# Memory attention of a sample group: split fp32r keys and values against unsplit fp32 in four column groups

## The chip, the core and the metric

The kernel runs on one core of one Trainium2 chip. The metric is device time in microseconds (us), the median of the runs of a kernel. A core has five engines that run side by side and meet at semaphores: TensorE (PE; its weight loads are shown as PEld), VectorE (DVE), ScalarE (ACT), GpSimd (POOL) and SyncE (SP), which here only starts transfers. Matmul results go to PSUM, of which eight banks of 128 x 512 fp32 exist in this program (the pool psp). All DMA queues share the core's 16 DMA engines.

## The reference, cut to what matters

One layer of a decoder is computed for a prompt of 256 tokens (TP) and a sample group of 8 sequences of 8 tokens (TS = 64 rows, NB = 8, LS = 8), with the same weights. The stage that changes is the cross-attention to 256 memory tokens per sequence, 4 heads of 512:

```python
def mem_attend(xn, k, v, wq, wo):
    q = (xn @ wq).reshape(b, L, MEM_HEADS, MEM_HEAD_DIM)
    s = jnp.einsum('blhd,bmhd->bhlm', q, k.astype(q.dtype)).astype(jnp.float32) * (1.0 / math.sqrt(MEM_HEAD_DIM))
    p = jax.nn.softmax(s, axis=-1)
    o = jnp.einsum('bhlm,bmhd->blhd', p.astype(v.dtype), v).reshape(b, L, D_MODEL)
    return (o @ wo).astype(xn.dtype)
```

For the prompt, k and v were computed earlier in the kernel and stand in DRAM (one sequence). For the sample they are inputs, cache_mem_k and cache_mem_v, eight sequences of 256 x 2048 fp32 each: a head of one sequence is 256 x 512, 512 KB.

## The kernel before, in words

**Precision.** TensorE takes fp32 operands in a slow form and fp32r operands (fewer mantissa bits) in a fast one. The kernel keeps fp32 accuracy by splitting a tile x into H = x as fp32r (an ACT copy) and L = x - H (a DVE subtraction), and by issuing three fp32r matmuls H*H, H*L, L*H for a product of two split operands. `split` (L246 to L249) does it; `high()` and `low()` give the buffers (seven each, HLB).

**The stream.** Work is fed to `Stream` (L58) as units of four parts: load (starts the weight DMA), first, second (preparations on DVE, ACT, POOL) and comp (matmuls). `add` runs a unit's load at once; the unit is prepared when more than `ahead` units stand behind it (WA = 3); its matmuls are issued when more than `room` prepared units of its kind wait (g for gemm units, a for attention units). Side generators (softmax, results) advance by one step with each unit whose matmuls are issued; `wait(n)` in them is n such steps. PE, ACT and DVE execute in exactly this program order.

**Units of the attention stage.** Four query panels qs (`panel`, L1095): 16 units of 128 rows of w_mem_q, each 12 matmuls of 320 columns (tile pg). The first panel runs alone; panels 1 to 3 stand between the keys of heads 0 to 2 (`between`). The first output panel o0, from w_mem_o, is handled in the same way around the keys of head 3 and the values after it. When a panel ends, `evac_q` (L1189) copies the queries out: the prompt's into qh and ql, the sample's, split, into qm, a zeroed matrix in which each sample's 8 query rows stand at their own columns, H beside L.

`kv_units` (L1275) makes two units of a 256 x 512 tile of keys or values. `kv_load` queues its load into one of four kv buffers (KVT): keys with four DMAs from SP, values with one from POOL; three are started ahead, then one with each tile used. For keys, DVE transposes 128 x 512 (tile tt, L1288). Then ACT makes KH (L1297) and DVE, or in 20 to 30% of the cases POOL (POOL_KV), makes KL (L1298). Prompt and sample go the same way.

`sample_scores` (L1321, tile pss): per sample and head, for each of four 128-wide pieces of the head, one matmul with KH and one with KL, 64 stationary columns from qm, 256 moving columns. `sample_softmax` adds the two halves with an fp32 matmul (psm), takes the softmax, transposes it and writes it, split, into pm (`split_diagonal`, L1178). `sample_values` (L1347, tile pso): two pieces of 128 tokens with VH and VL, 128 stationary columns of pm, 512 moving columns; `sample_result` adds up with another fp32 matmul (L1238). psp and po are the prompt's scores and values (three matmuls each). The values of a head run one head and LAG = 4 steps behind its keys; a step is one tile of keys and one of values.

After the stage, `residual_in` opens the next buffers and the rest of the output projection follows as ordinary gemm units (L367 to L369).

Of the kernel before, what the change touches and what calls it, by code (L numbers as in the profile page):

```python
# [57 lines left out]
class Stream:  # L58
# [105 lines left out]
def step(ctx, tc, ins, outs, dbg=None, stop=None):  # L164
# [79 lines left out]
    strm = Stream(WA, g=GD, a=KVB - 1)  # L244
# [15 lines left out]
    def rstd_of(pool, sq, n, count):  # L260
# [6 lines left out]
        t = pool.tile([P, n], F32, tag="rt", bufs=1, name="rt")  # L267
# [827 lines left out]
    def panel(w2d, c, ah, al, evac, wide=False):  # L1095
# [4 lines left out]
        def unit(k):  # L1100
# [20 lines left out]
            def comp():  # L1121
                if k == 0:
                    pts.extend(ps(f"pg{m}") for m in range(4))
# [15 lines left out]
    def open_tiles():  # L1139
# [3 lines left out]
        iv = ident.rearrange("p (b i q) -> p b i q", i=2, q=LS)  # L1143
        V.tensor_tensor(PQ["sel"].rearrange("p (b q) -> p b q", q=LS), iv[:, :, 0], iv[:, :, 1], ALU.add)
        PQ["half"] = pq.tile([TS, 2, TS], F32, name="half")
        zero = ident[0:TS, 0:TS].unsqueeze(1).broadcast_to([TS, 2, TS])
        S.activation(PQ["half"], zero, AF.Copy, scale=0.0)
        for g in range(2):
            V.tensor_copy(PQ["half"][:, g, 32 * g:32 * g + 32], PQ["sel"][0:TS, 0:32])
        for name, n, c in (("qm", 4, TS), ("pm", 2, P)):  # L1150
            t = pq.tile([P, n * NB, c], F32R, name=name)
            S.activation(t, ident[:, 0:c].unsqueeze(1).broadcast_to([P, n * NB, c]), AF.Copy, scale=0.0)
            PQ[name] = t
# [24 lines left out]
    def split_diagonal(t, src, n):  # L1178

        c = t.shape[2]  # L1180
        nb = c // 16
        for b0 in range(0, NB, nb):
            x = src[:, :, LS * b0:LS * (b0 + nb)].rearrange("p n (b q) -> p n b q", q=LS)
            hi, lo = (bass.AP(t.tensor, t.offset + c * b0 + LS * i, [list(t.ap[0]), [NB * c, n], [c + 16, nb], [1, LS]])
                      for i in range(2))
            S.activation(hi, x, AF.Copy)
            V.tensor_tensor(lo, x, hi.bitcast(F32), ALU.subtract)

    def evac_q(m, pt):  # L1189
        PQ.setdefault("parts", []).append(pt)  # L1190
        if m == 3:
            parts = PQ.pop("parts")
            qs = PQ["pool"].tile([P, 512], F32, tag="tt", bufs=TTB, name="qs")[:, 0:4 * TS].rearrange("p (j t) -> p j t", t=TS)
# [6 lines left out]
    def softmax(out, src, r):  # L1200
# [5 lines left out]
        V.scalar_tensor_tensor(m, m, -1.0, r, ALU.mult, ALU.mult)  # L1206
        for b in range(nb):
            S.activation(out[:, b], src[:, b], AF.Exp, bias=m[:, b:b + 1], scale=r[:, b:b + 1], accum_out=z[:, b:b + 1])
        V.reciprocal(z, z)
# [3 lines left out]
    def sample_softmax(sc, h):  # L1213
        pq = PQ["pool"]
        SC = pq.tile([P, 512], F32, tag="tt", bufs=TTB, name="SC")[0:TS]
        S.activation(SC, sc[0:TS], AF.Copy)
        yield from wait(3)
# [11 lines left out]
        split_diagonal(PQ["pm"], pt[:, 0:2 * TS].rearrange("p (m q) -> p m q", q=TS), 2)  # L1229
        yield 1  # L1230

    def sample_result(po, h):
        O = PQ["pool"].tile([P, 512], F32, tag="tt", bufs=TTB, name="O")
# [5 lines left out]
        split(AH[:, 4 * h:4 * h + 4, TP:T], AL[:, 4 * h:4 * h + 4, TP:T], pt[:, 0:4 * TS].rearrange("p (j t) -> p j t", t=TS))  # L1239
        yield 1  # L1240

    def prompt_softmax(sc, h):
        SP = PQ["pool"].tile([P, 2, TP], F32, tag="SP", bufs=1, name="SP")
        softmax(SP, sc.rearrange("p (b m) -> p b m", m=TP), PQ["r"][:, 0:2])
        yield from wait(6)
# [6 lines left out]
        split(PQ["ph"], PQ["pl"], pt.rearrange("p (m q) -> p m q", q=TP))  # L1252
        yield 1

    att_n = count(), count()
# [19 lines left out]
    def kv_units(src, keys, comp):  # L1275
# [4 lines left out]
        def unit(u):  # L1280
            def first():
                if u == 0:
                    next_load()
                    box["t"] = ready.popleft()
                t = box["t"]
                if keys:
                    tt = PQ["pool"].tile([P, 512], F32, tag="tt", bufs=TTB, name="tt")
                    V.transpose(tt.rearrange("p (k a i) -> p k a i", k=2, i=32),  # L1288
                                t.rearrange("p (a k j) -> p k a j", a=8, k=4)[:, 2 * u:2 * u + 2])
                    box[u] = tt  # L1290
                else:
                    box[u] = t[:, 512 * u:512 * u + 512]
# [128 lines left out]
    for _ in range(3):  # L1421
        strm.then(next_load)
# [700 lines left out]
```

## Time and profile before

| | us |
|---|---|
| median of 3 runs | 3209.01 (3207.13 to 3214.09) |
| profiled execution | 3211.91 |
| its span, first to last instruction | 3210.1 |
| busy: PE / DVE / ACT / POOL | 3138.9 / 2336.8 / 1631.5 / 1343.9 |
| mean granted TensorE clock | 0.989 |

Busy times are unions of what an engine executes. A matmul's busy time includes the way through the array and so overlaps with that of the next one; the pace of matmuls is read from start to start. An engine's idle time is put down to what ended it ("<-ACT KH L1297" is: until ACT had made KH). The granted clock falls for a while when TensorE has paused.

### The profile page before, as it was taken

The numbers are of one execution on the slowest core, as the hardware profiler recorded it, in microseconds if no ns is written. First come the engines' busy times: TensorE is split into PE (matmuls) and PEld (weight loads), VectorE is DVE, ScalarE is ACT, GpSimd is POOL, SyncE is SP. The second block draws the span as 40 slices with busy tenths as digits, with TensorE's granted clock in tenths as the row PEclk, the third lists the DMA queues.
The fourth block names the chain that finished last, engine by engine and source line by source line (L and its number), as shares of the span: only waits on it lengthen the run. The fifth ranks groups of instructions, "written<-read, shape, count | busy, mean of one in ns | idle before, by whom it ended". The sixth has DMA issues, their size and how long they took to land.

```text
span 3210.1 us, 57528 instructions
## 1 busy us (share of the span) xinstructions
PE 3138.9 (98%) x20589; PEld 2930.0 (91%) x20589; DVE 2336.8 (73%) x4551; ACT 1631.5 (51%) x3219; POOL 1343.9 (42%) x1438
## 2 busy tenths in 40 slices
PE   8999999999999999889999999999999999999997
PEld 7889999999999998779999999999999888888886
DVE  5556866666565557786688899987875888888885
ACT  6545543334454445555444444666664555555554
POOL 0002211111100001330138899988888555556552
PEclk9999999999999999989999999999999999999998
DMA  8668899899999988875676688878998989999995
GB/s 264 206 209 301 283 313 317 300 314 294 320 318 315 310 271 190 223 207 196 187 218 215 236 308 323 317 275 299 332 322 284 333 322 367 328 335 337 336 316 187
DMA packets 475372, 909.29 MB, mean 283 GB/s; under 512 B 40608, under 2 KB 286536, under 8 KB 449573
## 3 DMA queue, kind: packets, MB, share of 16 engines
q1 hardware_dynamic: 352972, 562.95, 52.7%
q0 software_dynamic: 54528, 208.44, 18.9%
q10 hardware_dynamic: 67584, 134.23, 12.3%
q8 instruction: 161, 2.64, 0.3%
q14 instruction: 127, 1.03, 0.1%
HBM read 849.41 MB, written 190.05 MB: 324 GB/s over the span
## 4 chain that ended last, share of the span: by engine, by line
PE 43%; DVE 2%; POOL 2%; issue 1%; DMA 1%; ACT 1%; DVEq 0%; POOLq 0%; SPq 0%; ACTq 0%
PE acc L2025 7%; PE acc L2026 7%; PE acc L2024 7%; PE pu L1871 6%; PE pu L1869 6%; PE pu L1870 6%; PE pgate L1775 2%; POOL L L1853 1%; DVE tt L1841 0%; PE pg L367 0%; PE pg L369 0%; PE pg L368 0%; DMA act_d<-at 0%; DVE gu L1733 0%; DVE L L249 0%
## 5 line engine op out<-in xcount | busy, mean ns | idle before, releaser
L249 DVE TENSOR_TENSOR L<-W,H 128x512 fp32r<-128x512 f32 x1320 | 912.0, 718 | 356.6 <-ACT H L248 350.7
L248 ACT ACTIVATE H<-W 128x512 fp32r<-128x512 f32 x1320 | 797.7, 625 | 673.9 <-PE acc L2026 237.3
L1853 POOL TENSOR_TENSOR L<-tt,H 128x512 fp32r<-128x512 f32 x509 | 645.1, 1297 | 76.6 <-ACT H L1850 67.8
L367 PE MATMUL pg<-AH,H 128*128 128x320 f32 (+1 forms) x1872 | 588.5, 314 | 1.7 <-ACT H L248 1.7
L1869 PE MATMUL pu<-XP,H 128*128 128x256 f32 x2048 | 585.6, 286 | 0.0
L1871 PE MATMUL pu<-XP,L 128*128 128x256 f32 x2048 | 580.4, 283 | 3.7 <-POOL L L1853 3.6
L369 PE MATMUL pg<-AH,L 128*128 128x320 f32 (+1 forms) x1872 | 579.7, 310 | 0.3 <-DVE L L249 0.3
L1870 PE MATMUL pu<-XP,H 128*128 128x256 f32 x2048 | 579.3, 283 | 0.0
L368 PE MATMUL pg<-AL,H 128*128 128x320 f32 (+1 forms) x1872 | 579.2, 309 | 0.0
L1841 DVE STREAM_TRANSPOSE tt<-W 128x512 f32<-128x512 f32 x512 | 338.1, 692 | 115.9 <-POOL L L1853 108.5
L2025 PE MATMUL acc<-L,wt 128*128 128x512 f32 x1024 | 399.0, 390 | 0.7 <-DVE L L249 0.6
L2024 PE MATMUL acc<-H,wt 128*128 128x512 f32 x1024 | 398.4, 389 | 0.0
L2026 PE MATMUL acc<-H,wt 128*128 128x512 f32 x1024 | 398.4, 389 | 0.0
L1871 PEld LDWEIGHTS pu<-XP,L 128*128 128x128 f32 x2048 | 392.7, 192 | 5.3 <-POOL L L1853 5.3
L1869 PEld LDWEIGHTS pu<-XP,H 128*128 128x128 f32 x2048 | 393.0, 192 | 0.2 <-issue 0.2
L1870 PEld LDWEIGHTS pu<-XP,H 128*128 128x128 f32 x2048 | 393.0, 192 | 0.0
L1850 ACT ACTIVATE H<-tt 128x512 fp32r<-128x512 f32 x512 | 307.0, 626 | 135.0 <-DVE tt L1841 105.1
L367 PEld LDWEIGHTS pg<-AH,H 128*128 128x128 f32 (+1 forms) x1872 | 351.2, 188 | 5.0 <-ACT H L248 2.2
L368 PEld LDWEIGHTS pg<-AL,H 128*128 128x128 f32 (+1 forms) x1872 | 351.4, 188 | 2.3
L369 PEld LDWEIGHTS pg<-AH,L 128*128 128x128 f32 (+1 forms) x1872 | 351.0, 187 | 1.5 <-DVE L L249 0.9
L1973 POOL TENSOR_TENSOR at<-at,G 128x108 f32<-128x108 f32 x192 | 165.3, 874 | 256.9 <-DMA at<-act_d 214.6
L2025 PEld LDWEIGHTS acc<-L,wt 128*128 128x128 f32 x1024 | 192.2, 188 | 42.7 <-DVE L L249 3.0
(485 smaller groups left out, 5291.7 us busy)
## 6 DMA issues: line engine op xcount, KB each, us to landing
u_d<-in_peer_u_dram ACTq DMA_DIRECT2D x128, 1024.0 KB
W<-u_d SPq DMA_DIRECT2D x128, 1024.0 KB
W<-in_peer_v_dram SPq DMA_DIRECT2D x256, 512.0 KB
W<-in_w_in_dram SPq DMA_DIRECT2D x176, 512.0 KB
W<-in_w_out_dram SPq DMA_DIRECT2D x64, 512.0 KB
W<-in_w_mem_k_dram SPq DMA_DIRECT2D x32, 512.0 KB
W<-in_w_mem_v_dram SPq DMA_DIRECT2D x32, 512.0 KB
W<-in_w_mem_q_dram SPq DMA_DIRECT2D x32, 512.0 KB
```

Of the source, the lines that this page charges most:

```text
L248: S.activation(h, src, AF.Copy)
L249: V.tensor_tensor(l, src, h.bitcast(F32), ALU.subtract)
L367: PE.matmul(out, hv[:, j, c0:c1], ah[:, k, 0:n], start=st, stop=False)
L368: PE.matmul(out, hv[:, j, c0:c1], al[:, k, 0:n], start=False, stop=False)
L369: PE.matmul(out, lv[:, j, c0:c1], ah[:, k, 0:n], start=False, stop=sp)
L1853: G.tensor_tensor(l, src, h.bitcast(F32), ALU.subtract)
L1869: PE.matmul(pu[:, 0:TP], hv[:, j], PP["xp"][:, 0, k], start=k == 0, stop=False)
L1870: PE.matmul(pu[:, 0:TP], hv[:, j], PP["xp"][:, 1, k], start=False, stop=False)
L1871: PE.matmul(pu[:, 0:TP], lv[:, j], PP["xp"][:, 0, k], start=False, stop=k == KC - 1)
L2024: PE.matmul(out, th, h, start=i == 0, stop=False)
L2025: PE.matmul(out, th, l, start=False, stop=False)
L2026: PE.matmul(out, tl, h, start=False, stop=i == P - 1)
```

## The change

The sample's keys and values are no longer split. Keys are transposed as a whole tile (128 x 1024, `turned`) and values are used as they were loaded; both go to TensorE as fp32, against fp32 queries (qm) and probabilities (pm) of 32 columns. The four 128-wide pieces of a head's keys are multiplied into four groups of 32 PSUM partitions (32j to 32j + 32), and so are the two token halves of two samples' values. A sample pair's values are issued when the second tile is there. The matrix half, now 128 rows, and sel add the groups up. The prompt's tiles are still split, into the common H and L buffers and without POOL. qm exists twice, for even and odd heads; SC and O share a buffer of their own. The softmax generators pause between their steps. Nine kv buffers take the place of four, four loads are started ahead in place of three; LAG is 3; within the stage five units stand ahead and room g is 4; room a is 2, later 3. Four units of o0 move ahead into the keys of head 3. A small buffer of `rstd_of` (rt) shares that of sq.

```diff
-HLB, KVB, GD, WA, WB = 7, 5, 6, 3, 4
-TU, AB, TTB, KVT, OB = 5, 3, 3, 4, 3
+HLB, GD, WA, WB = 7, 6, 3, 4
+TU, AB, TTB, KVT, OB = 5, 3, 3, 9, 3
-DW, XW, LAG = 8, 5, 4
+DW, XW, LAG = 8, 5, 3
-POOL_KV = 0.2, 0.3
+Q_AHEAD, Q_ROOM, KV_AHEAD = 5, 4, 4
...
-        if len(self.loading) > self.ahead:
+        while len(self.loading) > self.ahead:
...
-    strm = Stream(WA, g=GD, a=KVB - 1)
+    strm = Stream(WA, g=GD, a=2)
...
-        t = pool.tile([P, n], F32, tag="rt", bufs=1, name="rt")
+        t = pool.tile([P, n], F32, tag="sq", bufs=1, name="rt")
...
-        for name, n, c in (("qm", 4, TS), ("pm", 2, P)):
-            t = pq.tile([P, n * NB, c], F32R, name=name)
...
+        PQ["half"] = clear("half", [P, 2, TS])
+        V.tensor_reduce(PQ["half"][:, 0, 0:32], ident.rearrange("p (g r) -> p r g", r=32), AX.X, ALU.add)
+        V.tensor_copy(PQ["half"][:, 1, 32:64], PQ["half"][:, 0, 0:32])
+        PQ["qm"] = [clear(f"qm{i}", [P, 4 * NB, 32]) for i in range(2)]
+        PQ["pm"] = clear("pm", [P, 2 * NB, 32])
...
-                S.activation(qs[:, j], part[:, TP:T], AF.Copy)
-            split_diagonal(PQ["qm"], qs, 4)
+                S.activation(diagonal(PQ["qm"][h % 2], j, [[128, 2], [40, 4]]),
+                             part[:, TP:T].rearrange("p (a b q) -> p a b q", a=2, q=LS), AF.Copy)
...
         V.scalar_tensor_tensor(m, m, -1.0, r, ALU.mult, ALU.mult)
+        yield from wait(2)
         for b in range(nb):
             S.activation(out[:, b], src[:, b], AF.Exp, bias=m[:, b:b + 1], scale=r[:, b:b + 1], accum_out=z[:, b:b + 1])
+        yield from wait(2)
         V.reciprocal(z, z)
...
-        SC = pq.tile([P, 512], F32, tag="tt", bufs=TTB, name="SC")[0:TS]
-        S.activation(SC, sc[0:TS], AF.Copy)
-        yield from wait(3)
+        SC = pq.tile([P, 512], F32, tag="SO", bufs=1, name="SC")
+        S.activation(SC, sc, AF.Copy)
+        yield from wait(2)
...
-        SN = pq.tile([TS, 1, TP], F32, tag="SN", bufs=1, name="SN")
-        softmax(SN, pt[0:TS, 0:TP].unsqueeze(1), PQ["r"][0:TS, 2:3])
-        yield from wait(6)
+        yield 1
+        SN = nrm.tile([P, TP], F32, tag="ms", bufs=1, name="SN")[0:TS].unsqueeze(1)
+        yield from softmax(SN, pt[0:TS, 0:TP].unsqueeze(1), PQ["r"][0:TS, 2:3])
+        yield from wait(2)
...
-        split_diagonal(PQ["pm"], pt[:, 0:2 * TS].rearrange("p (m q) -> p m q", q=TS), 2)
+        for u in range(2):
+            S.activation(diagonal(PQ["pm"], u, [[72, 4], [32, 2]]),
+                         pt[:, u * TS:(u + 1) * TS].rearrange("p (x y q) -> p x y q", y=2, q=LS), AF.Copy)
...
-        O = PQ["pool"].tile([P, 512], F32, tag="tt", bufs=TTB, name="O")
+        O = PQ["pool"].tile([P, 512], F32, tag="SO", bufs=1, name="O")
...
-        softmax(SP, sc.rearrange("p (b m) -> p b m", m=TP), PQ["r"][:, 0:2])
-        yield from wait(6)
+        yield from softmax(SP, sc.rearrange("p (b m) -> p b m", m=TP), PQ["r"][:, 0:2])
+        yield from wait(3)
...
+    def next_tile():
+        next_load()
+        return ready.popleft()
+
+    def turned(t):
+        tt = PQ["pool"].tile([P, 1024], F32, tag="tt", bufs=TTB, name="tt")
+        V.transpose(tt.rearrange("p (k a i) -> p k a i", k=4, i=32), t.rearrange("p (a k j) -> p k a j", a=8, k=4))
+        return tt
...
             def second():
-                h, l = (PQ["pool"].tile([P, 512], F32R, tag=x, bufs=KVB, name=x) for x in ("KH", "KL"))
-                src = box.pop(u)
-                S.activation(h, src, AF.Copy)
-                (G if spread(next(att_n[keys]), POOL_KV[keys]) else V).tensor_tensor(l, src, h.bitcast(F32), ALU.subtract)
-                box["hl", u] = h, l
+                h, l = high(), low()
+                split(h, l, box["t"][:, 512 * u:512 * u + 512])
+                box[u] = h, l
...
         def sample_scores(b):
-                for j in range(2):
-                    q = PQ["qm"][:, (2 * u + j) * NB + b]
-                    for i, kk in enumerate((kh, kl)):
-                        PE.matmul(out, q, kk[:, TP * j:TP * j + TP], start=b % 4 == 0 and u == j == i == 0,
-                                  stop=b % 4 == 3 and u == j == i == 1)
+            kv_load(cache_k[0, b, :, h], True)
+            def first():
+                st["k", b] = turned(next_tile())
+            def comp():
+                tt = st.pop(("k", b))
+                for j in range(4):
+                    PE.matmul(st["ss"][32 * j:32 * j + 32, TP * (b // 4):TP * (b // 4) + TP], PQ["qm"][h % 2][:, j * NB + b],
+                              tt[:, TP * j:TP * j + TP], start=b % 4 == 0, stop=b % 4 == 3)
...
         def sample_values(b):
-                for i, vv in enumerate((vh, vl)):
-                    PE.matmul(st["so"], PQ["pm"][:, u * NB + b], vv, start=b == u == i == 0, stop=b == NB - 1 and u == i == 1)
+            def unit(i):
+                kv_load(cache_v[0, i, :, h], False)
+                def first():
+                    st["v", i] = next_tile()
+                def comp():
+                    if i == b:
+                        return
+                    vs = [st.pop(("v", n)) for n in (b, i)]
+                    for y, v in enumerate(vs):
+                        for u in range(2):
+                            g = 2 * y + u
+                            PE.matmul(st["so"][32 * g:32 * g + 32], PQ["pm"][:, u * NB + b + y], v[:, 512 * u:512 * u + 512],
+                                      start=b == 0, stop=b == NB - 2)
+                return None, first, None, comp, "a"
+            return [unit(b), unit(b + 1)]
...
-        between[3 * nk + LAG + 1 + i] = o0[2 * i:2 * i + 2]
-        between[4 * nk + LAG + 1 + 2 * i] = o0[8 + i:9 + i]
+        between[3 * nk + i] = o0[i:i + 1]
+        between[3 * nk + LAG + 1 + i] = o0[4 + i:5 + i]
+        between[4 * nk + LAG + 2 + 2 * i] = o0[8 + i:9 + i]
...
-                for u in range(2):
-                    steps += ks[u:u + 1] + bs[u:u + 1] + vs[u:u + 1]
-    for _ in range(3):
+            steps += ks + bs[:1] + vs + bs[1:]
+        if n == nk + LAG + 3:
+            steps.append(lambda: strm.room.update(a=3))
+    strm.then(lambda: strm.room.update(g=Q_ROOM))
+    strm.ahead = Q_AHEAD
+    for _ in range(KV_AHEAD):
         strm.then(next_load)
...
+    strm.ahead = WA
+    strm.then(lambda: strm.room.update(g=GD))
```

More of the change, by code (lines that the diff above doesn't have):

```diff
@@ L1093, in step, with panel @@
     strm.then(open_q)
-    def panel(w2d, c, ah, al, evac, wide=False):
+    def panel(w2d, c, ah, al, evac, wide=False, need=()):
         pts, box, units = [], {}, []
@@ L1121, in comp @@
             def comp():
+                assert all((n, k // 4) in done for n in need)
                 if k == 0:
@@ L1142, in open_tiles, with clear @@
         PQ["sel"] = pq.tile([P, TS], F32, name="sel")
[L1143 to L1149, printed above, removed]
-        for name, n, c in (("qm", 4, TS), ("pm", 2, P)):
-            t = pq.tile([P, n * NB, c], F32R, name=name)
-            S.activation(t, ident[:, 0:c].unsqueeze(1).broadcast_to([P, n * NB, c]), AF.Copy, scale=0.0)
-            PQ[name] = t
+        iv = ident.rearrange("p (y u x q) -> p y u x q", y=2, u=2, q=LS)
+        V.tensor_tensor(PQ["sel"].rearrange("p (x y q) -> p y x q", y=2, q=LS), iv[:, :, 0], iv[:, :, 1], ALU.add)
+        def clear(name, shape):
+            t = pq.tile(shape, F32, name=name)
+            S.activation(t, ident[:, 0:shape[2]].unsqueeze(1).broadcast_to(shape), AF.Copy, scale=0.0)
+            return t
+        PQ["half"] = clear("half", [P, 2, TS])
[3 more added lines that the diff above has]
+        PQ["pm"] = clear("pm", [P, 2 * NB, 32])
         PQ["qh"] = pq.tile([P, 4, TP], F32R, name="qh")
@@ L1176, in step, with diagonal, evac_q @@
     strm.then(open_tiles)
[L1178 to L1189, printed above, removed]
+    def diagonal(t, n, steps):
+        return bass.AP(t.tensor, t.offset + 32 * NB * n, [list(t.ap[0]), *steps, [1, LS]])
+    def evac_q(m, pt, h):
         PQ.setdefault("parts", []).append(pt)
@@ L1239, in sample_result @@
         split(AH[:, 4 * h:4 * h + 4, TP:T], AL[:, 4 * h:4 * h + 4, TP:T], pt[:, 0:4 * TS].rearrange("p (j t) -> p j t", t=TS))
+        done.add(("res", h))
         yield 1
@@ L1252, in prompt_softmax @@
         split(PQ["ph"], PQ["pl"], pt.rearrange("p (m q) -> p m q", q=TP))
+        done.add(("ph", h))
         yield 1
-    att_n = count(), count()
     loads = deque()
@@ L1273, in next_load, with prompt_units @@
             loads.popleft()()
-    def kv_units(src, keys, comp):
+    def next_tile():
[5 more added lines that the diff above has]
+        return tt
+    def prompt_units(src, keys, comp):
         kv_load(src, keys)
@@ L1381, in evac_o @@
         evac_next(XN["x"], k, pt, norm_sum(2), 4, BH, BL)
-    qs = [panel(w_mem_q[0], c, BH, BL, evac_q, wide=True) for c in range(4)]
-    o0 = panel(w_mem_o[0], 0, AH, AL, lambda m, pt: evac_o(m, pt))
+    qs = [panel(w_mem_q[0], c, BH, BL, lambda m, pt, c=c: evac_q(m, pt, c), wide=True) for c in range(4)]
+    o0 = panel(w_mem_o[0], 0, AH, AL, lambda m, pt: evac_o(m, pt), need=("res", "pv"))
     def residual_in():
@@ L1407, in step @@
             vs = tile_units(1, n - nk - LAG)
-            ks = tile_units(0, n)
-            if vs or n == 0:
-                steps += vs + ks[:1] + bs[:1] + ks[1:] + bs[1:]
-            else:
-                steps += bs + ks
+            steps += vs + bs + tile_units(0, n)
         else:
@@ L1415, in step @@
             vs = tile_units(1, n - nk - LAG)
-            if n < 4 * nk and n % nk == NB:
-                steps += ks + bs + vs
-            else:
-                for u in range(2):
-                    steps += ks[u:u + 1] + bs[u:u + 1] + vs[u:u + 1]
-    for _ in range(3):
+            steps += ks + bs[:1] + vs + bs[1:]
[4 more added lines that the diff above has]
+    for _ in range(KV_AHEAD):
         strm.then(next_load)
     for u in qs[0] + steps + o0[12:14]:
-        strm.add(*u)
+        if callable(u):
+            u()
+        else:
+            strm.add(*u)
+    strm.ahead = WA
+    strm.then(lambda: strm.room.update(g=GD))
     strm.then(residual_in)
```

45 lines of the change are left out of this document (18 added, 27 removed).

## The prediction

> **What bounds the kernel now.** I read the page first. TensorE is busy nearly throughout and the chain that ended last is mostly TensorE, so time is gained only where TensorE waits or where it is given less to stream. The clock line dips once, near the middle.
>
> ```profile
> span 3210.1 us, 57528 instructions
> PE 3138.9 (98%) x20589; PEld 2930.0 (91%) x20589; DVE 2336.8 (73%) x4551; ACT 1631.5 (51%) x3219; POOL 1343.9 (42%) x1438
> PEclk9999999999999999989999999999999999999998
> PE 43%; DVE 2%; POOL 2%; issue 1%; DMA 1%; ACT 1%; DVEq 0%; POOLq 0%; SPq 0%; ACTq 0%
> ```
>
> Next the timeline gave the borders of the attention stage (first matmul of the query panel, L1128; first matmul of the gemm behind the panels, L367), and the table by stretches its inside (columns after the span: busy time of PE, PEld, DVE, ACT, POOL; granted clock, DMA share, GB/s).
>
> ```profile
> 1176.31 0.31 PE L1128 MATMUL pg<-BH,H 128*128 128x320 f32 x1
> 1466.75 0.31 PE L367 MATMUL pg<-AH,H 128*128 128x320 f32 x1
> 1176.00:1466.00 290.00, 261.16 (x1613) 236.42 (x1612) 214.59 (x366) 161.85 (x327) 74.16 (x76) 0.92 0.78 214
> 1202.00:1240.00 38.00, 36.45 (x261) 35.99 (x260) 31.98 (x51) 20.92 (x43) 6.46 (x5) 1.00 1.07 222
> 1300.00:1400.00 100.00, 82.41 (x466) 70.51 (x465) 75.07 (x129) 55.17 (x120) 28.96 (x30) 0.86 0.76 201
> 1466.00:1560.00 94.00, 94.00 (x643) 93.83 (x642) 55.44 (x100) 46.13 (x87) 0.00 (x0) 1.00 0.51 165
> 500.00:600.00 100.00, 100.00 (x726) 98.09 (x726) 61.65 (x136) 38.49 (x71) 16.20 (x31) 1.00 0.94 318
> ```
>
> The stage lasts 1466.75 - 1176.31 = 290.4 us; TensorE is idle for about 29 of them and the clock averages 0.92, where the stretch behind it has no idle time at clock 1.00. The groups by form inside the stage, and two timelines for the pace, give what TensorE has to stream.
>
> ```profile
> L1128 PE MATMUL pg<-BH,H 128*128 128x320 f32 x256 | 82.3, 322 | 7.9 <-ACT SP L1208 3.8 <-ACT H L248 3.0 <-DVE ql L249 1.1
> L1321 PE MATMUL pss<-KH,qm 128*64 128x256 f32 x128 | 36.3, 302 | 2.2 <-DVE qm L1187 1.6 <-ACT KH L1297 0.6
> L1321 PE MATMUL pss<-KL,qm 128*64 128x256 f32 x128 | 35.9, 300 | 4.6 <-POOL KL L1298 3.0 <-DVE KL L1298 1.5
> L1347 PE MATMUL pso<-KL,pm 128*128 128x512 f32 x64 | 27.8, 435 | 5.2 <-DVE KL L1298 3.2 <-POOL KL L1298 2.0
> L1347 PE MATMUL pso<-KH,pm 128*128 128x512 f32 x64 | 27.2, 425 | 3.9 <-ACT KH L1297 3.9
> L1128 PE MATMUL pg<-AH,H 128*128 128x320 f32 x64 | 20.4, 319 | 0.5 <-ACT AH L248 0.5
> L1337 PE MATMUL psp<-KL,qh 128*128 128x256 f32 x32 | 10.0, 313 | 1.2 <-DVE KL L1298 1.1
> L1361 PE MATMUL po<-pl,KH 128*128 128x256 f32 x32 | 9.3, 291 | 0.0
> L1220 PE MATMUL psm<-SC,half 64*64 64x256 f32 x16 | 4.3, 389 | 0.1
> L1238 PE MATMUL pso<-sel,O 128*128 128x64 f32 x32 | 5.1, 312 | 0.2 <-ACT O L1234 0.2
> ```
>
> ```profile
> 1279.08 0.39 PE L1347 MATMUL pso<-KH,pm 128*128 128x512 f32 x1
> 1279.31 0.39 PE L1347 MATMUL pso<-KL,pm 128*128 128x512 f32 x1
> 1279.54 0.28 PE L1321 MATMUL pss<-KH,qm 128*64 128x256 f32 x1
> ...
> 1280.01 0.31 PE L1128 MATMUL pg<-BH,H 128*128 128x320 f32 x1
> ...
> 1281.77 0.39 PE L1347 MATMUL pso<-KH,pm 128*128 128x512 f32 x1
> ```
>
> ```profile
> 1246.52 0.31 PE L1130 MATMUL pg<-BH,L 128*128 128x320 f32 x1
> 1246.76 1.07 PE L1220 MATMUL psm<-SC,half 64*64 64x256 f32 x4
> 1247.76 0.41 PE L1128 MATMUL pg<-BH,H 128*128 128x320 f32 x1
> 1248.01 0.31 PE L1129 MATMUL pg<-BL,H 128*128 128x320 f32 x1
> ```
>
> Pace, from start to start: twelve 320-column matmuls take 1281.77 - 1280.01 = 1.76 us, 0.147 each; four of 256 columns 1280.01 - 1279.54 = 0.47, 0.1175 each; one of 512 columns 0.23. **The floor of the stage**: panels (3 x 256 + 3 x 64 = 960) 141.1; sample scores (256) 30.1; sample values (128) 29.4; prompt scores and values (6 groups of 32) 22.6; the small fp32 matmuls about 10 (two rows of 4.3 and 5.1 busy). Sum 233. So 57 of the 290 us are waits and a lowered clock. Of the 28.8 us of idle time, 15.9 stand before the four sample rows (2.2 + 4.6 + 5.2 + 3.9), nearly all for KH or KL, the split halves.
>
> **The change, part by part.** *The split goes.* Of 144 half tiles, 128 are the sample's; only the prompt's 16 are still split.
>
> ```profile
> L1297 ACT ACTIVATE KH<-tt 128x512 fp32r<-128x512 f32 x72 | 45.5, 631 | 60.5 <-DVE tt L1288 57.9 <-PE pso L1347 1.5 <-PE pss L1321 1.0
> L1297 ACT ACTIVATE KH<-kv 128x512 fp32r<-128x512 f32 x72 | 43.3, 623 | 12.7 <-DMA kv<-in_cache_mem_v_dram 8.6 <-PE pso L1347 2.0 <-PE pss L1321 1.9
> L1298 DVE TENSOR_TENSOR KL<-kv,KH 128x512 fp32r<-128x512 f32 x58 | 43.3, 761 | 8.8 <-ACT KH L1297 7.9 <-issue 0.7
> L1298 DVE TENSOR_TENSOR KL<-tt,KH 128x512 fp32r<-128x512 f32 x51 | 35.7, 699 | 10.4 <-ACT KH L1297 10.1
> L1298 POOL TENSOR_TENSOR KL<-tt,KH 128x512 fp32r<-128x512 f32 x21 | 27.0, 1286 | 105.6 <-ACT KH L1297 100.5 <-PE pss L1321 5.1
> L1288 DVE STREAM_TRANSPOSE tt<-kv 128x512 f32<-128x512 f32 x72 | 50.6, 702 | 1.5 <-DMA kv<-out_dram 1.1 <-issue 0.3
> POOL kv L1267 <- DVE KL L1298: 46.4, 18, 5.1
> ACT H L248 <- DMA W<-in_w_mem_q_dram: 17.2, 10, 3.3
> ```
>
> ACT loses 128 x 0.627 = 80 of its 162 us. DVE loses 43.3 + 35.7 less 16 x 0.7 = 68 of 215; POOL loses all its subtractions. No other engine then stands near TensorE's load, so this part is worth waits alone. Transposes: 72 of 512 columns become 36 of 1024, the same elements, an estimated 1.4 us each (2 x 702 ns); an L behind one waits up to 0.7 us longer, covered by the deeper queue (five units ahead in place of three); without that cover 36 x 0.7 = 25 us at most.
>
> *TensorE streams something else.* Scores: eight split matmuls of a (head, sample) become four unsplit fp32 ones, one per group of 32 columns, 256 moving columns each. Values: eight split matmuls of a sample pair become four fp32 ones of 512. An fp32 matmul is two instructions: psm is called twice for each of four heads and has 16 rows. One of them is busy 376 ns at 256 columns (1.07 us for four is three paces and one such end), 0.10 more than a 256-column split one's 0.28; so a slot is 0.1175 + 0.097 = 0.214 us, and at 512 columns twice that, 0.428.
>
> What four groups cost together, no row shows. Lower end: all four stream at once and the two instructions take two slots: 32 x 0.43 + 16 x 0.86 = 27 us. Upper end: one after another, eight slots: 32 x 1.71 + 16 x 3.42 = 110 us. I take five slots. TensorE starts its matmuls in order in every timeline above, and the two instructions of one fp32 matmul stand one behind the other and use the same columns; the second must wait for the first, and what may overlap is the second of one group with the first of the next: 1 + 3 + 1 slots. That is 32 x 1.07 + 16 x 2.14 = 68.5 us against 59.5 now, 9 us more. The Trainium skill ("TensorE: Matmul & The Clock Gate", section on packing small matmuls) reports 2.38 times for three column tiles and a strict order of starts; by its plain packing rule the sum would be the lower end.
>
> *Changing the array's shape.* About 48 stretches of 32-column work stand between 128-column work. Bounds: nothing, as between pss (128*64) and its neighbours (1279.54 and 1280.01 are full pace on both sides); or the psm case (64*64): 0.24 in place of 0.147 before it, 1.00 - 4 x 0.214 = 0.14 inside it, and 0.25 in place of 0.147 behind it, some 0.34 in all: 48 x 0.34 = 16 us. The nearer row is pss, which uses all 128 rows too: I take nothing and keep 16. The skill says ("TensorEngine Tiling (Array Packing)", Key Properties) that a change of tiling mode drains TensorE; the pss rows do not show it, the psm rows may; by that rule the sum is 16 us higher.
>
> *The softmax is cut up* with pauses, so that panel splits run between its steps; it aims at the 3.8 us that a panel waits behind ACT's SP. The sample's keeps nine pauses in all, the prompt's gets seven for six. The first values of a head now stand five steps behind its last sample keys (six before, LAG 4 to 3), some four units each, so twenty pops for nine pauses: nothing. Were that cover gone, four heads would each wait for the tail of a softmax chain; the dearest such wait in the rows above is the 3.8 us.
>
> *Small things.* SC and O share one buffer of their own; O of a head is read long before the next SC. rt shares sq's buffer, SN the old ms: used in other stretches, nothing. The zeroing and the query diagonals (8 + 8 small instructions, 4 + 4 for pm) shrink by 2 to 4 us on ACT and DVE, off the path. Four units of the output panel o0, with their weight loads on SP, move ahead into head 3's keys; none is added. By the code the loads are the same in number on both queues (values on POOL, keys and weights on SP), and none is moved past the other queue's; a value load leaves earlier, as POOL no longer stands in a subtraction or waits for KL's buffer release (46.4 us); nine buffers let keys and the weights behind them on SP leave earlier too (17.2 us of ACT).
>
> **DMA**: 0.78 x 290 = 226 us of full share. Below some 226/0.94 = 240 us (the share held at 500 to 600) transfers bind; at the 1.07 of 1202 to 1240, 211.
>
> **Sum.** Floor 233 + 9 = 242. Of the 57 lost, 55% (15.9 of 28.8) went with the split halves; of the remaining 26 the deeper queue and the cut softmax take some, DMA at 226/261 = 0.87 share gives some back: 19 (8 to 30). Stage 261, 29 us less. The profiled execution took 3211.9, 2.9 over the median 3209.0 of the runs; on the median: 3180, own range 3165 to 3205 with the bounds of shape changes and waits.
>
> **The rivals.** *Four at once* (24%): floor 242 - 41 = 201; transfers then bind at 211 to 240, I take the upper end, since the first panel's 28 us (16 x 1.76) have few cache loads to fill them: 50 us less, 3159. For it: groups use different columns and different PSUM partitions. Against: the order of instructions. *A drain at every change of shape* (12%): 261 + 16 = 277, 3196. *No overlap* (24%), the other side: eight slots on L1321's and L1347's successors, floor 242 + 41 = 283, and with 17 of waits 300: 10 us more, 3219. It decides from about seven slots on: 233 - 59.5 = 173.5 us of the floor are not the sample's, so the stage keeps its 290 when the sample takes 290 - 173.5 - 19 = 97, and a slot of all units is 13.7 us: 7.1 slots. For it: every row shows matmuls streaming one at a time; against: nothing in the trace forbids it. That the change does nothing for the time is this case with nearly all waits gone, 283 + 8 = 291: within 0.2%, about what a measurement of this kernel can tell from no change.
>
> **How the numbers follow.** Forecast 40%, rivals 24, 12, 24. Faster: 38 + 24 + 9 + 1 = 72%; within 0.2%: 2 + 3 + 6 = 11%; slower 17%. The range 3145 to 3220 leaves out half of *no overlap* and a little of *four at once*.
>
> **What would show it.** Starts of the score matmuls: pairs 0.21 us apart are five slots, four starts within some ns two slots, 0.21 for every single one eight. KH and KL vanish but for 32 rows; ACT and DVE fall to about 80 and 145 us; the clock rises to 0.97 or more. The prediction is wrong if slots differ, if a new wait (pm late, W late) fills what KL left, or if the clock stays low because narrow matmuls count for less.

## The result, and the profile after

The changed kernel takes 3176.8 us (median of four runs, 3166.7 to 3182.2) against 3211.6 for the kernel before in the same comparison (3207.1 to 3219.2): ratio 0.9886, 95% interval 0.9851 to 0.9921. A second comparison gave 3171.7 against 3207.9, ratio 0.9893 (0.9870 to 0.9916). So the change saves about 35 us. The profiled execution took 3166.7, 10 us under the median, so the difference between the two profiles (45.2 us) is some 10 us larger than that between the medians.

From the page of the kernel after: the totals, the clock line and the chain by engine.

```profile
span 3164.9 us, 57035 instructions
PE 3100.0 (98%) x20589; PEld 2878.4 (91%) x20589; DVE 2256.1 (71%) x4410; ACT 1558.0 (49%) x3088; POOL 1305.0 (41%) x1403
PEclk9999999999999999999999999999999999999998
PE 42%; DMA 2%; POOL 2%; issue 2%; DVE 2%; ACT 1%; SPq 0%; DVEq 0%; POOLq 0%; ACTq 0%
```

TensorE issues the same 20589 matmuls, and the dip of the clock line is gone. The timeline gives the stage's borders (first two rows) and one stretch of sample scores.

```profile
1173.52 0.31 PE L1129 MATMUL pg<-BH,H 128*128 128x320 f32 x1
1421.53 0.31 PE L367 MATMUL pg<-AH,H 128*128 128x320 f32 x1
...
1205.64 0.31 PE L1130 MATMUL pg<-BL,H 128*128 128x320 f32 x1
1205.79 0.31 PE L1131 MATMUL pg<-BH,L 128*128 128x320 f32 x1
1206.03 1.07 PE L1322 MATMUL pss<-tt,qm 128*32 128x256 f32 x16
1207.03 0.41 PE L1129 MATMUL pg<-BH,H 128*128 128x320 f32 x1
1207.28 0.31 PE L1130 MATMUL pg<-BL,H 128*128 128x320 f32 x1
1207.43 0.31 PE L1131 MATMUL pg<-BH,L 128*128 128x320 f32 x1
```

The stage is 1421.53 - 1173.52 = 248.0 us where it was 290.4. From its end to the end of the span there are 1743 us in both traces, so 42.4 of the 45.2 us lie in the stage. The other 2.8 lie ahead of it, where the profiles of the changed kernel and its variants scatter by more (the stage begins at 1169.8 to 1174.1 us in them). Sixteen score instructions (two samples, four groups, two instructions each) go by in 1207.03 - 1206.03 = 1.00 us.

The table by stretches (busy time of PE, PEld, DVE, ACT, POOL; clock; DMA share; GB/s), then the groups by form and the waits inside the stage:

```profile
1173.00:1421.00 248.00, 224.12 (x1616) 185.27 (x1615) 134.07 (x224) 87.47 (x196) 28.21 (x41) 0.96 1.02 245
1200.00:1240.00 40.00, 40.00 (x300) 34.92 (x299) 22.23 (x33) 12.95 (x29) 1.46 (x2) 1.00 1.12 234
1360.00:1420.00 60.00, 48.23 (x332) 36.48 (x331) 26.45 (x43) 18.88 (x39) 11.32 (x17) 0.91 0.83 253
1421.00:1510.00 89.00, 89.00 (x609) 89.00 (x608) 52.87 (x96) 43.36 (x83) 0.00 (x0) 1.00 0.52 163
```

```profile
L1322 PE MATMUL pss<-tt,qm 128*32 128x256 f32 x256 | 19.8, 390 | 1.8 <-DVE tt L1280 1.8
L1362 PE MATMUL pso<-kv,pm 128*32 128x512 f32 x128 | 16.8, 604 | 0.0
L1129 PE MATMUL pg<-BH,H 128*128 128x320 f32 x256 | 83.0, 324 | 0.8 <-ACT SP L1201 0.4 <-ACT SN L1201 0.3 <-DVE ql L249 0.2
L1131 PE MATMUL pg<-AH,L 128*128 128x320 f32 x64 | 21.4, 334 | 8.3 <-DVE L L249 8.3
L248 ACT ACTIVATE H<-W 128x512 fp32r<-128x512 f32 x80 | 46.8, 628 | 86.4 <-DMA W<-in_w_mem_q_dram 66.7 <-DMA W<-in_w_mem_o_dram 10.8 <-PE pss L1322 4.2
L1280 DVE STREAM_TRANSPOSE tt<-kv 128x1024 f32<-128x1024 f32 x36 | 44.7, 1241 | 40.1 <-DMA kv<-in_cache_mem_k_dram 21.5 <-DMA kv<-out_dram 11.5 <-PE pss L1322 3.7
```

```profile
ACT H L248 <- DMA W<-in_w_mem_q_dram: 66.7, 16, 12.0
DVE tt L1280 <- DMA kv<-in_cache_mem_k_dram: 21.5, 8, 6.4
PE pg L1131 <- DVE L L249: 9.3, 3, 6.1
PE ppp L241 <- DVE AL L249: 9.2, 1, 9.2
```

Read them together. The sample rows of TensorE have 1.8 us of idle time before them; four rows had 15.9. Yet TensorE is still idle for 248 - 224.1 = 23.9 us at clock 0.96, above all late (48.2 of 60 us busy from 1360 on), while behind the stage it has no gap at clock 1.00. The waits have moved: ACT now waits 66.7 us for query weights (17.2 before), the subtraction of L follows late, and TensorE waits behind it. Two waits make up most of the idle time. Before the 9.2 us one (a transpose, ppp) ACT stood 12.0 us at a load of query weights, until 1307.75; the subtraction AL, which the view names, came only after that. In the 6.1 us one L stood on DVE behind a transpose that had waited 7.1 us for a load of the prompt's keys. The DMA share, 1.12 while TensorE is still full at 1200 to 1240, is 1.02 over the stage (a share over 1 is possible: it adds up the times of packets under way). By these rows the stage has turned from one limited by preparation into one limited by transfers. Which transfers, and what TensorE would do without them, took the experiments.

### The profile page after: what moved, and what is told of

It reads as the page before. It is cut to its first block, busy times and chain, and to the rows that moved or that the text cites. A ratio compares the mean times of both kernels' runs of the same rounds, so it can differ in the third digit from the quotient of the medians.

```text
span 3164.9 us, 57035 instructions
## 1 busy us (share of the span) xinstructions
PE 3100.0 (98%) x20589; PEld 2878.4 (91%) x20589; DVE 2256.1 (71%) x4410; ACT 1558.0 (49%) x3088; POOL 1305.0 (41%) x1403
## 4 chain that ended last, share of the span: by engine, by line
PE 42%; DMA 2%; POOL 2%; issue 2%; DVE 2%; ACT 1%; SPq 0%; DVEq 0%; POOLq 0%; ACTq 0%
PE pu L1895 7%; PE pu L1893 7%; PE pu L1894 7%; PE acc L2049 6%; PE acc L2050 6%; PE acc L2048 6%; PE pgate L1799 2%; POOL L L1877 1%; DMA gv<-in_peer_v_dram,EV 1%; DMA at<-act_d 1%; DVE tt L1865 0%; PE pg L367 0%; PE pg L369 0%; PE pg L368 0%; DVE gu L1757 0%
## 5 line engine op out<-in xcount | busy, mean ns | idle before, releaser
L249 DVE TENSOR_TENSOR L<-W,H 128x512 fp32r<-128x512 f32 x1320 | 900.4, 710 | 341.2 <-ACT H L248 335.5
L367 PE MATMUL pg<-AH,H 128*128 128x320 f32 (+1 forms) x1872 | 588.0, 314 | 0.0
L367 PEld LDWEIGHTS pg<-AH,H 128*128 128x128 f32 (+1 forms) x1872 | 350.9, 187 | 2.8
L1997 POOL TENSOR_TENSOR at<-at,G 128x108 f32<-128x108 f32 x192 | 173.9, 919 | 240.3 <-DMA at<-act_d 183.5
```

Source lines behind the costliest of these rows:

```text
L249: V.tensor_tensor(l, src, h.bitcast(F32), ALU.subtract)
L367: PE.matmul(out, hv[:, j, c0:c1], ah[:, k, 0:n], start=st, stop=False)
```

## The experiments

The first set asks how TensorE streams the four groups and what limits the stage now. The stage times below run from the first panel matmul to the first L367 of each trace.

**Two samples' scores, group by group, and a control.** Both issue two samples' scores together; they differ in the order alone.

```diff
 # order
+for j in range(4):
+    for c in (b - 1, b):
 # pair
+for c in (b - 1, b):
+    for j in range(4):
```

> The scores of two samples are issued together, group by group: both samples' matmuls of column group 0, then both of group 1, and so on; nothing is left out. In the changed kernel the eight instructions of a sample's scores took two slots of 0.215 us (starts of the four groups 7 ns apart). Theory A, each column group has a queue of its own: the pair still takes four slots, 0.86 us. Theory B, TensorE starts instructions in program order and the changed kernel is lucky in that order: a group's four instructions go one behind another and only the last of a group overlaps with the first of the next, 13 slots, 2.8 us per pair, 16 x 1.9 = 31 us more for TensorE. If transfers bind the stage, A leaves the time as it is (3160 to 3185) and B adds less than 31 us, since the stage has some 38 us of gaps.

> The same two samples together, but sample by sample, the order of the changed kernel; nothing is left out. It is the control for the run in group order: four slots per pair under both theories. It has 16 stretches of 32-column score work in place of 32. If a change of the array's shape costs 0.3 us for both ways, as the starts around these stretches suggest (0.24 before, 0.31 and 0.25 behind, in place of 0.147, 0.215 and 0.147), TensorE has 16 x 0.3 = 4.7 us less to do; if transfers bind the stage, the time stays within 5 us of the changed kernel (3165 to 3185).

From the timeline of the first one:

```profile
1210.78 0.31 PE L1131 MATMUL pg<-BH,L 128*128 128x320 f32 x1
1211.01 1.09 PE L1324 MATMUL pss<-tt,qm 128*32 128x256 f32 x16
1212.04 0.42 PE L1129 MATMUL pg<-BH,H 128*128 128x320 f32 x1
```

Sixteen instructions in 1.03 us, against 1.00 sample by sample. The starts within the stretch are at 1211.014, .028, .041, .054, then .254, .470 and .686: four slots, 13 ns between groups; sample by sample it was 7 ns (1206.031, .037, .044, .051, the second instructions from .271). One run each took 3168.3 and 3170.8 (stages of 251.9 and 256.5 us). So the order of issue hardly matters, as theory A had it: each column group streams its own instructions one behind the other, beside the other three. Both have fewer stretches of narrow work (28 for scores and values together, against 41), but no gain from that shows in one run each.

**All groups on one.** A unit's four score matmuls go to one group, and value pairs use two groups in place of four.

```diff
-PE.matmul(st["ss"][32 * j:32 * j + 32, ...], ..., start=b % 4 == 0, stop=b % 4 == 3)
+PE.matmul(st["ss"][32 * r:32 * r + 32, ...], ..., start=j == 0, stop=j == 3)      # r = b % 4
-g = 2 * y + u
+g = 2 * y + b // 2 % 2
```

> The changed kernel with the column groups taken out of the overlap, nothing left out: the four matmuls of a sample's scores go to one group (that of sample b is b mod 4), where they add up, and the two token halves of a sample's values go to one group too. The matrices half and sel add the groups up as before. A score unit should take eight slots of 0.215 us in place of two, a value pair four of 0.43 in place of two: 32 x 1.29 + 16 x 0.86 = 55 us more for TensorE, whose pace was 220 us in the run with large key rows (2.3 us idle, full clock). Theory A, the overlap of the groups is what makes the unsplit form worth it: the stage goes to 275 to 285 us and the ratio to before to 0.995 to 1.001. Theory B, transfers hide most of it: stage 255 to 265, ratio 0.988 to 0.994.

```profile
1209.17 0.31 PE L1131 MATMUL pg<-BH,L 128*128 128x320 f32 x1
1209.41 1.91 PE L1323 MATMUL pss<-tt,qm 128*32 128x256 f32 x8
1211.25 0.41 PE L1129 MATMUL pg<-BH,H 128*128 128x320 f32 x1
```

```profile
1170.00:1439.00 269.00, 267.00 (x1617) 203.79 (x1616) 133.91 (x225) 88.05 (x196) 28.20 (x41) 1.00 0.92 227
```

Eight instructions take 1.84 us, eight slots of 0.215 and 0.12 more at the end. TensorE is now busy nearly without a gap (2.0 us idle) at clock 1.00, and it sets the stage: 268.9 us, 21 more than with the overlap. The kernel takes 3188.5 against 3207.9, ratio 0.9945 (0.9930 to 0.9959). Stage and ratio lie between the two theories: the overlap saves 21 of TensorE's own 49 us (267 against 218, from the run with whole rows below), as the faster kernel waits 30 us and this one 2. And this kernel still beats the one before: with every slot of the scores paid in full it comes out ahead.

**Whole rows for the keys.** One load in place of four; rows of 2048 bytes in place of 512. The elements then stand in the wrong order, so the kernel is a test and not a version to use.

```diff
-for b in range(4):
-    nc.sync.dma_start(t[32 * b:32 * b + 32].rearrange(...), src[:, P * b:P * b + P].rearrange(...))
+nc.sync.dma_start(t.rearrange("p (m d) -> p m d", m=2), src.rearrange("(m p) d -> p m d", p=P))
```

> A tile of keys is loaded with one DMA in whole 2 KB rows, as values are, in place of four DMAs in rows of 512 B; the scores are then of a wrong order of elements, all instructions and bytes stay. In the changed kernel 36864 packets of 512 B take 45 ns each, 104 us of all 16 DMA engines' time in a stage of 248 us; packets of 2 KB take 84 to 117 ns. Theory A, the stage is bound by the transfers and by their small packets: 9216 packets of some 100 ns are 58 us, 46 us less, and the stage falls to TensorE's pace, some 210 to 222: 26 to 38 us faster than the changed kernel, ratio to before 0.977 to 0.981. Theory B, bytes bind, not packets: within 5 us of the changed kernel, ratio 0.987 to 0.990. The run cannot tell small packets from the four places that four DMAs take among the eight that SP may have under way; the run with keys from two queues can.

```profile
1173.00:1393.00 220.00, 217.69 (x1615) 181.23 (x1614) 132.28 (x223) 87.71 (x196) 28.22 (x41) 1.00 0.79 275
```

Stage 220.1 us, 28 less; TensorE idle 2.3, clock 1.00, share 0.79; 3140.1 us, ratio 0.9783 (0.9764 to 0.9802). Worked out from the packet records of the traces, times on each of the 16 engines on average: in the changed kernel's stage the keys are 36864 packets of 512 bytes at 45 ns, 105 us; values are 4608 of 4096 bytes at 224 ns, 65 us; weights some 9000 of 2048 bytes at 117 ns, 66 us. As 2048-byte packets at 94 ns the keys' 9216 cost 54 us. The sum of all packets falls from 253 to 173 us. So theory A holds: the changed kernel's stage is set by its transfers, and 220 is TensorE's own pace for the new work. Two things change together here, the length of the rows and the number of loads (36 in place of 144).

**Half of the values not loaded.**

```diff
-kv_load(cache_v[0, i, :, h], False)
+if i == b: kv_load(cache_v[0, i, :, h], False)
```

> Half of the sample's value loads are left out: the second sample of a pair uses the first one's tile. All matmuls stay. That is 4 x 4 x 512 KB = 8.4 MB of some 60 MB that the stage moves in 248 us (245 GB/s). Theory A, transfers bind the stage after the change: it loses 8.4 MB / 245 GB/s = 34 us, down to the pace of TensorE of some 210, so 25 to 34 us: ratio to before 0.977 to 0.981. Theory B, the 38 us of gaps come from the order of softmax, splits and matmuls: under 6 us, ratio 0.987 to 0.990.

```profile
1172.00:1410.00 238.00, 224.42 (x1617) 184.59 (x1616) 132.81 (x224) 87.34 (x195) 16.94 (x25) 0.97 0.96 220
```

Stage 237.9, 10 less; 3155.3 us, ratio 0.9843 (0.9816 to 0.9871). A pure count of bytes would have given 34 (8.4 MB at 246 GB/s). The packet time fell by 25 us (1.02 x 248 to 0.96 x 238), and the stage by 10: the 512-byte packets stood at 46 ns still and the keys kept their 105 us. The result lies between the two theories. Bytes alone do not set the stage; what holds the other 15 us, this run does not settle.

**Who issues, and in what order.** First two of the four loads of each key tile through POOL's queue in place of SP's; then the panel weights through ACT's.

```diff
 # kpool
-nc.sync.dma_start(t[32 * b:32 * b + 32]...)
+(nc.sync if b < 2 else nc.gpsimd).dma_start(t[32 * b:32 * b + 32]...)
 # wact (panel weights)
-nc.sync.dma_start(...)
+nc.scalar.dma_start(...)
```

> Of the four DMAs of a tile of keys, two are issued from POOL, which has been left with the values' loads; nothing is left out. SP waits some 70 us for earlier transfers of its own before it can issue the next key load (39.5 behind weights, 31.1 behind keys). Theory A, small packets bind the DMA engines: the time stays within 5 us of the changed kernel, ratio 0.986 to 0.991. Theory B, the number of DMAs that SP may have under way binds: SP's waits halve and the stage loses 10 to 25 us, ratio 0.979 to 0.985.

> The panels' weight loads are issued from ACT in place of SP, so that they no longer stand behind the key loads; nothing is left out. In the changed kernel ACT waits 66.7 us for weights of the panels. Theory A, transfers bind and a weight load that leaves earlier delays the caches' by as much: within 5 us, ratio 0.986 to 0.991. Theory B, the order on SP is what costs: 5 to 20 us faster, ratio 0.981 to 0.986. Slower than the changed kernel would mean that ACT, which executes in order, now stands at a weight load.

```profile
1171.00:1421.00 250.00, 227.30 (x1617) 188.60 (x1616) 133.48 (x224) 87.07 (x196) 70.14 (x113) 0.95 1.03 243
```

```profile
DVE tt L1280 <- DMA kv<-in_cache_mem_k_dram: 54.9, 15, 7.6
ACT H L248 <- DMA W<-in_w_mem_q_dram: 29.8, 11, 6.3
```

The stretch is that of the keys on POOL's queue: stage 249.8, ratio 0.9868 (0.9845 to 0.9890). Its queues, first in the changed kernel's stage and then in this run's (packets, MB, share; q1 is SP's queue, q0 POOL's):

```profile
q1 hardware_dynamic: 50892, 39.41, 72.6%
q0 software_dynamic: 5696, 21.20, 28.9%
```

```profile
q1 hardware_dynamic: 31206, 29.75, 55.8%
q0 software_dynamic: 9149, 30.63, 46.5%
```

This run changed more than its expectation saw. By the packet records POOL's queue moves eight rows of a partition as one packet of 4096 bytes: 18432 packets of 512 bytes are left, and 2304 of 4096 stand for the others. SP's waits for earlier transfers before a key load fell from 70.6 to 32.5 us (21.7 behind weights, 10.8 behind keys). Still the packet time stayed at 257 us, and nothing was gained. So neither the relief of SP's queue nor half as many 512-byte packets brought any of the 28 us of the whole rows. What is left of the things that whole rows changed is the length of the rows in memory, which are still 512 bytes here; a run that changes the row length alone was not made.

The waits above are those with the weights on ACT's queue: the wait for weights falls from 66.7 to 29.8 and the wait for keys rises from 21.5 to 54.9; stage 254.6, ratio 0.9895 (0.9861 to 0.9929). Neither differs from the changed kernel by more than its interval. With the weights moved, the place in the queue decides which load is late, and not how late they are together.

**Buffers and the split, each undone.** First four cache buffers in place of nine; then eight, with the subtraction and copy of each sample half tile done into scratch that nobody reads; then both.

```diff
 # bufs4
-KVT 9, KV_AHEAD 4
+KVT 4, KV_AHEAD 3
 # dummy: KVT 8; dummy4: KVT 4, KV_AHEAD 3; both:
+def second():
+    for u in range(2):
+        extra(tile[:, 512 * u:512 * u + 512])     # split into EH, EL
```

> The changed kernel with four cache buffers and three loads ahead, as before the change; nothing is left out. Theory A, transfers bind and nine buffers keep them going: with four, the value tiles that wait for their pair hold back the loads, the DMA share of the stage falls to about 0.8 as before, and 15 to 35 us of the gain go: ratio 0.992 to 1.000. Theory B, buffers do not matter because the engines' relief made the gain: ratio 0.987 to 0.991.

> The changed kernel with the splits of the sample's keys and values put back as work whose results nobody reads: 128 ACT copies and 128 DVE subtractions of 128x512, into two small buffers of their own; there are eight cache buffers in place of nine to make room. ACT goes from 88 to some 168 us of the stage, DVE from 134 to 222 of 248. Theory A, the engines' relief is part of the gain: DVE at 90% in order delays transposes, weight splits and softmax, 10 to 30 us slower than the changed kernel, ratio 0.992 to 1.000. Theory B, the gain came from TensorE's streaming and the buffers alone, and transfers hide the splits: within 5 us, ratio 0.987 to 0.991.

> The splits put back as work that nobody reads, and four cache buffers with three loads ahead: of the change only TensorE's new streaming and the new order of units are left. The stage took 248 us with the change, 258 with the splits put back (eight buffers), 273 with four buffers, 290 before. Theory A, splits and buffers cost by themselves and add up or more: 283 to 295 us, ratio 0.997 to 1.003; what TensorE saves is then hidden by waits. Theory B, the buffers alone decide and the splits hide behind the loads: 270 to 278 us, ratio 0.992 to 0.996.

Their stretches, one fence each in that order:

```profile
1173.00:1446.00 273.00, 240.19 (x1613) 193.07 (x1612) 132.67 (x223) 87.78 (x196) 26.64 (x38) 0.94 0.90 221
```

```profile
1172.00:1430.00 258.00, 232.99 (x1617) 191.44 (x1616) 215.81 (x352) 159.21 (x325) 28.27 (x41) 0.94 0.97 235
```

```profile
1172.00:1455.00 283.00, 240.36 (x1605) 195.02 (x1605) 215.40 (x349) 157.66 (x323) 28.12 (x41) 0.92 0.83 212
```

| | ratio to before | us saved, of 3209 | stage of the profiled run |
|---|---|---|---|
| changed kernel | 0.9893 (0.9870 to 0.9916) | 34 | 248.0 |
| four buffers | 0.9939 (0.9918 to 0.9960) | 20 | 273.4 (a run 13 over its median) |
| split kept, eight buffers | 0.9919 (0.9899 to 0.9938) | 26 | 258.0 |
| split kept, four buffers | 0.9986 (0.9971 to 1.0001) | 4 | 284.6 |

With four buffers the DMA share of the stage is 0.90, not the 0.8 of theory A, though the ratio is in its range; with both undone it is 0.83, and TensorE is idle for 43 us. With both undone nearly nothing is left, although TensorE still has the new, shorter work. With the split kept, the buffers are worth 26 - 4 = 22 us; with four buffers, the absent split is worth 20 - 4 = 16; together 30. The copies' share with many buffers, 34 against 26, has intervals that overlap. The scratch has two buffers for its high parts and one for its low ones, where the kernel before had five of each, which may hold back ACT and DVE more than the real split did; its price is rather an upper one.

**Half of the keys in whole rows.** If short rows bind, TensorE can turn some keys itself: keys of samples 0, 2, 4 and 6 of each head are loaded as 2048-byte rows, put in order by two copies on ACT, and turned by eight TensorE transposes and two evacuations.

```diff
+wide = b in (0, 2, 4, 6)
+if wide: nc.sync.dma_start(t.rearrange("p (m d) -> p m d", m=2), src.rearrange("(m p) d -> p m d", p=P))
...
+transpose(pt[:, P * y:P * y + P], tt[:, 512 * x + P * y:512 * x + P * y + P])     # 8 per tile, psum "pkt"
```

> An attempt at a faster version, nothing left out: every second sample's keys are loaded in whole 2 KB rows with one DMA, put in the query's order of elements by ACT (two copies of 128x512) and transposed by TensorE (eight 128x128 transposes through PSUM, then one copy by ACT and one by DVE) in place of DVE; its scores are issued with those of the next sample. In the run with large rows for all 36 key tiles the DMA engines' time fell from 253 to 174 us, 2.2 us a tile, and TensorE then set the pace at 220 us. Theory A, small packets bind: 16 tiles take 35 us off the DMA engines' time (218 us); TensorE's pace rises by 128 transposes of 0.11 us and falls by 16 shape changes of 0.3, to 230: stage 232 to 240, 8 to 16 us faster than the changed kernel, ratio 0.982 to 0.986. Theory B, the transposes break the stream (PSUM banks, ACT in order) or small packets were not it: no faster, 0.987 or above.

> The changed kernel itself, on the same chip and beside the same runs of the kernel before, for the comparison with the faster version: ratio 0.985 to 0.992.

```profile
1174.00:1410.00 236.00, 230.76 (x1742) 196.89 (x1742) 126.85 (x223) 112.43 (x244) 28.21 (x41) 1.00 0.94 258
```

```profile
L1345 PE MATMUL pss<-tt,qm 128*32 128x256 f32 x256 | 19.2, 385 | 1.8 <-ACT tt L1340 0.9 <-DVE tt L1338 0.9
L241 PE MATMUL pkt<-ident,tt 128*128 128x128 f32 x128 | 16.7, 273 | 0.0
```

Stage 236.3 us, in theory A's range, although TensorE is given 16.7 us (busy) more; idle 5.2, clock 1.00. The median is 3160.0, ratio 0.9843 (0.9820 to 0.9865); the changed kernel beside it had 3171.7, 0.9893 (0.9870 to 0.9916). This version beats both kernels by its own comparison, though the two intervals are close.

## Why the prediction was right and where it was not

**The total.** Time, sign and range held: 3180 forecast, 3177 and 3172 measured. The stage was forecast 29 us shorter and is 42 shorter in the profile, about 35 by the medians. But the time came out near by two errors of opposite sign, which is luck: the floor was put at 242 and is 218 (220.1 less 2.3 idle, in the run with whole rows), and the waits at 19 and are 30 (248 - 218). Of the recorded cases it is the rival *four at once* that tells what happened, TensorE faster and transfers binding; its 3159 is 18 us too low, as it let the transfers bind at 240 us, where the stage takes 248.

**Five slots: wrong.** The failed step is "the second must wait for the first, and what may overlap is the second of one group with the first of the next". The measured starts are 7 ns apart for four groups, so two slots. In the run with whole rows, where TensorE hardly waits, the score rows take 18.3 us from start to next start, the value rows 16.5, and the panel matmuls beside them 7.1 more than their pace (next paragraph): 41.9 us, some 18 below the 59.5 of before, where I had added 9. The slot itself (0.214 us) was right: from the second start to the third it is 0.215. The mistake was to read the order of starts in rows that all used the same columns. In the run group by group the first matmul of the second group, the third in program order, starts 13 ns behind the first one, while a group comes to its own next start only 0.24 us later; so the strict order of starts that the prediction quotes does not hold across groups here. The lower end, the rival *four at once*, was the right one for TensorE. The packing rule of the Trainium skill ("TensorE: Matmul & The Clock Gate", section on packing small matmuls) gave that end, and the trace agrees with it, with 7 ns a group.

**Shape changes: a term put at nothing that cost some 14 us.** I took nothing, from the 64-column rows, and kept 16 as a bound. Before the scores stand 0.24 us in place of 0.147 (1206.03 - 1205.79), behind them 0.25 (1207.28 - 1207.03), and the stretch is 0.14 longer than four slots of 0.215: 0.33 us in all. The trace has 41 stretches of 32-column work (26 of scores, 15 with values) rather than 48: 14 us. The part ahead of and behind 36 of them shows in the panel matmuls, the 7.1 us above; the part inside is contained in the 18.3 and 16.5.

That the shape is the cause is not shown. The changed kernel's psm rows are fp32 too, on 64 columns and all 128 rows, the shape of the old pss rows:

```profile
1279.00 0.28 PE L1340 MATMUL psp<-H,ql 128*128 128x256 f32 x1
1279.21 1.08 PE L1214 MATMUL psm<-SC,half 128*64 128x256 f32 x4
1280.21 0.39 PE L1338 MATMUL psp<-H,qh 128*128 128x256 f32 x1
1280.44 0.28 PE L1339 MATMUL psp<-L,qh 128*128 128x256 f32 x1
```

They pay 0.21 ahead and 0.23 behind in place of 0.12, and 1.00 for four slots of 0.215: 0.33 us again. The old pss rows, fp32r on this shape, paid nothing. So narrow columns alone cost nothing, and what the costly rows (32 columns, 64 columns, and the 64*64 psm of before) have in common is fp32 on narrow columns between fp32r rows. Which part of that costs, no run separates. The rows to price by were those of the same number format, and they gave 0.34. The Trainium skill's drain at a change of mode ("TensorEngine Tiling (Array Packing)", Key Properties) would fit the 128*32 rows, but the trace does not show that it is this drain.

**Floor of the stage.** 233 - 59.5 + 18.3 + 16.5 = 208 against 218 measured. Of the 10 us between them, 7.1 are the panel matmuls at the borders of the narrow stretches; the prompt's rows take 24.6 us where I had 22.6, and the small fp32 matmuls 11.6 where I had 10. The run with all groups on one is short in the same way (173.5 + 56.0 + 26.8 = 256 against 267).

**The split's waits: right in kind, the size is shared.** With both undone (split kept, four buffers) 4 us are left of 34: the 18 us of TensorE's work alone are worth almost nothing. The idle time before the sample's rows fell from 15.9 to 1.8 us. ACT and DVE are at 87 and 134 us (about 80 and 145 forecast). But the gain needs the nine buffers as much as the absent split; I had given the queue only part of 26 us.

**Transfers: named, but as a bound of the wrong kind.** I expected 0.94 of a share of 226 us to bind at 240 if TensorE got fast. The stage is at 248 with share 1.02: 253 us of packet time for 60.9 MB, where it was 227 for 62.1. In the denser stage each packet takes longer (512 bytes 45 ns in place of 40, 4096 bytes 224 in place of 193), so share is not an amount of work that a shorter stage merely squeezes. "W late", listed as what could make the prediction wrong, is the largest new wait, and late transfers cost about 28 us of the 70 that TensorE's pace would have given (290 to 220). The clock stayed at 0.96, below the 0.97 forecast: it is 1.00 in the three kernels whose TensorE idled 2 to 5 us, narrow matmuls included, so it follows the waits.

**No overlap: its sum is near, by two errors again.** For the run with eight slots for the scores and four for the values the rival's terms give 173.5 + 55 + 27 + 17 = 273, and 268.9 were measured: TensorE's part is 267, not 256, and the waits are 2, not 17. The term that failed is the waits: when TensorE's work grows, the others have time, and the wait for preparation does not add to it. Eight slots for the values too would bring 27 us more, 296, about the rival's 300; that is worked out, not run.

**The softmax, the moved panel units and the small things** showed little: panel matmuls wait less than 1 us for SP (3.8 before), and the time outside of the stage is the same within 3 us.

## What to carry to other kernels

Ask what each of the other resources does at the new pace before summing a gain: here TensorE's work fell by some 18 us and its waits for the split went, and the short rows of the keys then took 28 us back. Price transfers by the time of their packets in the trace, not by bytes or by a share, and let a run decide what makes them long: half as many small packets gained nothing, whole rows 28 us. Price a new row by rows of the same number format as well as of the same shape. The waits of a stage are no constant of it: with TensorE's work longer they fell to 2 us, with it shorter they rose to 30.

## What the runs showed of the hardware

Four column groups of 32 run fp32 matmuls side by side, in both orders of issue that were tried: starts 7 ns apart sample by sample, 13 ns group by group. A stretch of fp32 matmuls on 32 columns, or on 64, between fp32r ones on 128 cost about 0.33 us beyond its slots. fp32r matmuls on 64 columns between such ones on 128 cost nothing: in the kernel before, the panel matmuls at these borders keep their 0.147 us within 3 ns in the median.

In the changed kernel's stage a 512-byte packet took 45 ns on average (40 to 49 in the other runs), a 2048-byte one 117 and a 4096-byte one 224: 11, 18 and 18 GB/s while it is under way. With whole rows a 2048-byte one took 94 ns, 22 GB/s, with the same bytes in the stage. The Trainium skill ("DMA: Bandwidth & Descriptors", the table at its head) puts the line rate at 512 bytes and more; in these runs 512-byte packets stay well below the longer ones of the same stage.
